# Three weight blocks in place of two through the token quarters of a decoder trunk's opening

## The chip, the cores and the metric

The kernel runs on one core of a Trainium2 chip. The metric is device time in microseconds of one execution; a kernel's time is the median of several runs. Engines have short names: PE is TensorE (matmul), PEld its weight load, DVE is VectorE, ACT is ScalarE, POOL is GpSimd, SP is SyncE, which only issues transfers (DMAs). Each engine works through a queue of its own in written order, and a transfer is issued by SP, ACT or POOL at its place in that engine's queue.

## What is computed

One layer of a hybrid decoder trunk over 1024 prompt tokens and 32 sample tokens of width 1024, cut to what matters here:

```python
h = rmsnorm(x, norm_w)                 # per token: x * rsqrt(mean(x*x) + eps) * w
z = h @ w_in                           # one projection, split into
# q, k, v of a window attention (A), q, k, v of three dilated groups (B),
# pooling inputs (C), gates, merge gates
s = q @ k.T / 8 + bias                 # bias: ALiBi distance and the window's mask
p = softmax(s); o = p @ v              # per head and block of 128 queries
m = sigmoid(ma) * (oa*silu(ga) @ wa) + sigmoid(mb) * (ob*silu(gb) @ wb) + sigmoid(mc) * (oc*silu(gc) @ wc)
y = rmsnorm(x + m @ w_out, final_norm_w)
# further outputs: the last K, V rows of the prompt, and the sample's state
# buffers shifted by four rows, which is a copy from memory to memory
```

## The kernel before, in words

**Data.** A float32 value is kept as two parts, a rounded one (hi) and the rest (lo), so every product takes three matmuls: hi x hi, hi x lo, lo x hi. Tokens stand transposed in `xh` and `xl` (8 blocks of 128 features by 1056 tokens). `w_in` comes as 58 blocks of 1024 x 128. Block 0 is K and block 1 is V of branch A, blocks 2 to 5 are Q of head pairs 0 to 3. A block is loaded to `w_raw` (`w_load`) and split by `w_split`: ACT writes `w_hi`, DVE (in the opening POOL) subtracts to get `w_lo`.

**A projection.** `proj_chunk` multiplies one block with a range of tokens: 24 matmuls into one PSUM bank (tag `pj`, three banks). For blocks 0 and 1 they run part by part: 8 with hi and `xh`, 8 with hi and `xl`, 8 with lo and `xh`; such eight are called a third here. `project(n, ...)` runs a block over three chunks of 384, 384 and 288 tokens.

**The opening** (from L967 on). The 1056 tokens are nine tiles. A tile is loaded (`x_tile`), squared and summed on ACT (`x_sq`, L272) with two small steps on POOL for the reciprocal root (L273, L274), scaled on DVE in two halves (`x_scale`, L282), and turned on PE by eight transposes (`x_turn`, L293), after which ACT copies `xh` out of PSUM (L295) and DVE makes `xl` (L296). Projections need whole quarters: 256, 256, 256 and 288 tokens, two tiles each and three in the last. K and V go through the quarters in turn, and between their chunks the next tiles are squared, scaled and turned. What comes out of a K chunk goes through `evac_k`, which alternates ACT and DVE four times; POOL copies the result to the other half of the partitions. After the opening `project(2)`, Q of pair 0, runs alone.

**Around it.** Two token tiles share each of two pairs of buffers, so SP asks for a tile when an earlier one has been scaled. `make_bias(pair)` has SP load the bias of a pair (256 KB). `state_copy` has POOL issue the memory-to-memory copies of the sample's buffers, 511 KB each; eight of them stand next to each other in POOL's queue behind two small memsets of `up` that end the opening. `later(k, f)` runs `f` after k ticks, a tick being six matmuls of a projection; attention is interleaved with projections by ticks too. Attention of pair 0 starts three ticks into `project(3)`: four matmuls for a block's scores (`emit_s`, L505, two PSUM banks), a minimum with the bias on DVE (L509), an exponential on ACT (L512), transposes (L525) and the product with V (L547).

Of the kernel before, what the change touches and what calls it, by code (L numbers as in the profile page):

```python
# [96 lines left out]
def build(tc, x_p, x_s, w_in, w_pr, w_out, nw, fnw, sink, sinkrow, w_pool, pscale, st_a, st_b1, st_b2, st_b3, st_c,  # L97
# [35 lines left out]
    def w_load(n):  # L133
        if n >= len(seq) or n in raws:
            return
        kind, i = seq[n]
        raw = wr.tile([128, 8, 128], F32, tag="raw", name="w_raw", bufs=2)
        (sp if n == 0 else act).dma_start(out=raw, in_=(w_in if kind == "in" else w_pr)[i])
        raws[n] = raw

    def w_split(n, eng=dve):
        if n >= len(seq) or n in splits:
            return
        w_load(n)
        raw = raws[n]
        if seq[n][0] == "in":
            hi = wr.tile([128, 8, 128], F32R, tag="whi", name="w_hi", bufs=2)
            lo = wr.tile([128, 8, 128], F32R, tag="wlo", name="w_lo", bufs=2)
            act.activation(out=hi, in_=raw, func=AF.Copy)  # L149
            eng.tensor_tensor(out=lo, in0=raw, in1=hi.bitcast(F32), op=ALU.subtract)  # L150
        else:
            hi = wp_pool[0].tile([128, 8, 128], F32R, tag="phi", name="p_hi")
            lo = wp_pool[0].tile([128, 8, 128], F32R, tag="plo", name="p_lo")
            act.activation(out=hi, in_=raw, func=AF.Copy, scale=0.25)
            dve.scalar_tensor_tensor(out=lo, in0=raw, scalar=0.25, in1=hi.bitcast(F32), op0=ALU.mult, op1=ALU.subtract)
        splits[n] = (hi, lo)
# [96 lines left out]
    xh = xtp.tile([128, 8, NT], F32R, tag="xh", name="xh")  # L253
    xl = xtp.tile([128, 8, NT], F32R, tag="xl", name="xl")
    gc1_cm, gc1 = open_pool("gc1")
    up = [gc1.tile([128, 16 + NT], F32, tag=f"c{t}", name=f"up{t}") for t in range(2)]
    at_cm, at0 = open_pool("attn")
    nwb = at0.tile([128, D], F32, tag="bias", name="nwb", bufs=2)

    def x_tile(i):  # L260
        rows = 128 if i < 8 else NS
        xt = at0.tile([128, D], F32, tag=f"q{i % 2}", name="x_nat", bufs=2)
        sp.dma_start(out=xt[:rows], in_=x_p[i * 128:(i + 1) * 128, :] if i < 8 else x_s)
        return xt

    def x_sq(i):
        rows = 128 if i < 8 else NS
        xt = xtiles.pop(i)
        sq = [at0.tile([128, 512], F32, tag="os" if i % 3 == 2 else "e", name="sq", bufs=2 if i % 3 == 2 else 4) for _ in range(2)]
        junk = at0.tile([128, D], mybir.dt.bfloat16, tag="pt", name="junk", bufs=5)  # L270
        ss = at0.tile([128, 2], F32, tag="ss", name="ss", bufs=3)
        act.activation(out=junk[:rows], in_=xt[:rows], func=AF.Square, accum_out=ss[:rows, 0:1])  # L272
        pool.tensor_scalar(out=ss[:rows, 1:2], in0=ss[:rows, 0:1], scalar1=1.0 / D, scalar2=EPS, op0=ALU.mult, op1=ALU.add)  # L273
        pool.tensor_tensor(out=ss[:rows, 0:1], in0=ss[:rows, 1:2], in1=mhalf[:rows], op=ALU.pow)  # L274
        xnorm[i] = xt, sq, ss

    def x_scale(i):
        rows = 128 if i < 8 else NS
        xt, sq, ss = xnorm.pop(i)
        for h in range(2):  # L280
            hs = slice(512 * h, 512 * h + 512)
            dve.scalar_tensor_tensor(out=sq[h][:rows], in0=xt[:rows, hs], scalar=ss[:rows, 0:1], in1=nwb[:rows, hs], op0=ALU.mult, op1=ALU.mult)  # L282
        xscaled[i] = sq

    def x_turn(i):
        rows = 128 if i < 8 else NS
        sq = xscaled.pop(i)
        c0 = i * 128
# [12 lines left out]
    def proj_chunk(n, c0, cn, tag="pj"):  # L301
        hi, lo = splits[n]
        ps = bank(tag)
        parts = ((hi, xh), (hi, xl), (lo, xh))
        order = [(k, p) for p in range(3) for k in range(8)] if n < 2 else [(k, p) for k in range(8) for p in range(3)]
        for step, (k, p) in enumerate(order):
            pe.matmul(ps[:, :cn], lhsT=parts[p][0][:, k, :], rhs=parts[p][1][:, k, c0:c0 + cn], start=(step == 0), stop=(step == 23))  # L307
            if step % 6 == 5:
                yield None
        yield ps  # L310

# [653 lines left out]
        dve.tensor_scalar(out=nsinkrow, in0=sinkrow_sb, scalar1=-1.0, scalar2=None, op0=ALU.mult)  # L965

    warm = bank("o")  # L967
    xtiles[0] = x_tile(0)
    sp.dma_start(out=nwb, in_=bass.AP(tensor=nw.tensor, offset=nw.offset, ap=[[0, 128], [1, D]]))
    xtiles[1] = x_tile(1)  # L970
    w_load(0)
    xtiles[2] = x_tile(2)
    raws[1] = at0.tile([128, 8, 128], F32, tag="bias", name="w_raw1", bufs=2)
    sp.dma_start(out=raws[1], in_=w_in[1])
    xtiles[3] = x_tile(3)
    for _ in range(28):
        pe.transpose(warm[:, 0:128], ident, ident)
    at[0] = at0
# [2 lines left out]
    x_sq(1)  # L981
    x_scale(1)
    x_turn(0)
    w_split(0, pool)
    x_turn(1)
    x_sq(2)
    x_scale(2)
    x_sq(3)
    w_split(1, pool)
    ek, ev = evac_k(0), evac_v(0)  # L990
    nxt_s, nxt_t = 3, 2
    for c0, cn in ((0, 256), (256, 256), (512, 256), (768, 288)):
        for w, e in ((0, ek), (1, ev)):
            if nxt_s < 9:
                if nxt_s + 1 < 9:
                    xtiles[nxt_s + 1] = x_tile(nxt_s + 1)
                x_scale(nxt_s)
                if nxt_s + 1 < 9:
                    x_sq(nxt_s + 1)
                nxt_s += 1  # L1000
            if (c0, w) == (0, 1):
                w_load(2)
            if (c0, w) == (256, 1):
                small_loads()
# [12 lines left out]
    side.append(attention())
    for i in range(4):
        make_bias(i)
        if i >= 2:  # L1020
            flush_attention(i - 2)
        project(2 + i, evac_q(i), 1.6, 2 if i else 0)
    for pr in range(6):
        pair = 4 + pr
        make_bias(pair)
# [445 lines left out]
```

## Time and profile before

| | |
|---|---|
| time, median of 3 runs | 1083.14 us (1082.66 to 1086.08) |
| the profiled execution's own time | 1084.24 us |
| its span in the trace | 1082.5 us |
| PE busy | 1045.4 us, 97% |
| DVE, ACT, POOL busy | 435.5, 343.9, 195.8 us |
| mean granted clock of PE | 0.99 |

The profiled execution is one more run, with the profiler on; its span is what the trace covers. A row of the timeline gives start, duration, engine, line and operation with its output and inputs, and in brackets how long the engine had been idle and what ended that. PE's matmuls are pipelined, so a row's duration is longer than the time for which it holds the engine; the distance between starts tells that.

### The profile page before, as it was taken

What the parts mean: (1) busy time and instruction counts of PE and PEld (TensorE: products, weight loads), DVE (VectorE), ACT (ScalarE), POOL (GpSimd) and SP (SyncE); (2) the same over time, 40 slices, a digit from 0 to 9 for tenths busy, and PEclk for the clock granted to TensorE, in tenths of its full rate; (3) what the DMA queues carried; (4) which work ended last, traced back from release to release, by engine and by line L of the source; (5) the groups of instructions that cost most, each with busy time, mean ns of one, the idle gap of its engine ahead of it and who ended that gap; (6) DMA issues with size and microseconds to landing.
All of it is one profiled execution on the core that took longest, in us unless ns stands there. A gap on an engine that the chain in (4) does not pass through costs nothing.

```text
span 1082.5 us, 18049 instructions
## 1 busy us (share of the span) xinstructions
PE 1045.4 (97%) x7421; PEld 994.4 (92%) x7421; DVE 435.5 (40%) x960; ACT 343.9 (32%) x888; POOL 195.8 (18%) x303
## 2 busy tenths in 40 slices
PE   7999999999999999979999899999999999999996
PEld 7998999999999999968979899999999999998884
DVE  5656654544435343474224641222122221346331
ACT  5456543544535244222211311111112121243221
POOL 5400030211303030300003460311113021111011
PEclk8999999999999999999999999999999999999998
DMA  7241133425254453527568853454143240332221
GB/s 258 79 161 59 60 126 115 149 71 184 70 176 131 124 179 113 160 80 260 194 235 208 256 167 117 164 167 136 60 135 131 83 159 33 92 116 89 100 83 58
DMA packets 54574, 144.42 MB, mean 133 GB/s; under 512 B 13030, under 2 KB 29732, under 8 KB 53156
## 3 DMA queue, kind: packets, MB, share of 16 engines
q1 hardware_dynamic: 41980, 65.28, 19.5%
q0 software_dynamic: 2816, 44.87, 12.2%
q10 hardware_dynamic: 9696, 33.12, 9.9%
q8 instruction: 58, 0.95, 0.4%
q14 instruction: 24, 0.20, 0.1%
HBM read 127.65 MB, written 60.55 MB: 174 GB/s over the span
## 4 chain that ended last, share of the span: by engine, by line
PE 83%; DMA 7%; DVE 5%; ACT 2%; POOL 1%; SPq 1%; issue 1%; POOLq 0%; ACTq 0%; DVEq 0%
PE ps_pj L307 53%; PE ps_pj L1342 5%; PE ps_s L1342 4%; PE ps_s L1207 4%; PE ps_t L1207 4%; PE ps_s L505 3%; PE ps_o L547 3%; PE ps_t L525 2%; DMA w_in<-w_scr 2%; POOL o_in L1134 1%; DMA w_raw<-in_w_in 1%; DMA w_in<-rz_scr 1%; DMA kv<-in_kt_b 1%; PE ps_o L860 1%; DMA o_in<-o_scr 1%
## 5 line engine op out<-in xcount | busy, mean ns | idle before, releaser
L307 PE MATMUL ps_pj<-xh,w_hi 128*128 128x384 f32 (+2 forms) x1408 | 461.7, 335 | 6.4 <-ACT xh L295 3.0
L307 PE MATMUL ps_pj<-xh,w_lo 128*128 128x384 f32 (+2 forms) x1408 | 443.9, 322 | 5.2 <-DVE w_lo L150 5.1
L307 PE MATMUL ps_pj<-xl,w_hi 128*128 128x384 f32 (+2 forms) x1408 | 444.4, 322 | 0.0
L307 PEld LDWEIGHTS ps_pj<-xh,w_hi 128*128 128x128 f32 x1408 | 263.2, 190 | 16.1 <-issue 6.3
L307 PEld LDWEIGHTS ps_pj<-xh,w_lo 128*128 128x128 f32 x1408 | 261.6, 188 | 6.4 <-DVE w_lo L150 6.0
L307 PEld LDWEIGHTS ps_pj<-xl,w_hi 128*128 128x128 f32 x1408 | 262.7, 189 | 0.7 <-issue 0.3
L150 DVE TENSOR_TENSOR w_lo<-w_raw,w_hi 128x1024 fp32r<-128x1024 f32 x55 | 67.3, 1224 | 204.6 <-ACT w_hi L149 197.0
L1216 ACT ACTIVATE mth<-ps_pj 128x384 f32<-128x384 f32 (+1 forms) x72 | 33.4, 464 | 257.3 <-PE ps_pj L307 250.3
L1224 POOL TENSOR_TENSOR m<-m,mth 128x384 f32<-128x384 f32 (+1 forms) x48 | 47.8, 1012 | 275.4 <-DVE mth L1222 274.9
L397 POOL TENSOR_SCALAR k<-k 64x384 fp32r<-64x384 f32 (+1 forms) x44 | 20.1, 458 | 298.4 <-ACT k L393 298.1
L512 ACT ACTIVATE e<-e,nm_b 128x256 f32<-128x256 f32 (+1 forms) x96 | 44.2, 461 | 62.9 <-DVE nm_b L509 62.6
L149 ACT ACTIVATE w_hi<-w_raw 128x1024 fp32r<-128x1024 f32 x57 | 60.1, 1054 | 1.0 <-DMA w_raw<-in_w_in 1.0
L357 DVE SCALAR_TENSOR_TENSOR q<-ps_pj,q 64x384 fp32r<-64x384 f32 (+1 forms) x60 | 30.7, 512 | 60.2 <-ACT q L356 60.1
L505 PE MATMUL ps_s<-k,q 128*128 128x256 f32 x320 | 51.6, 285 | 0.9 <-DVE nm_a L509 0.9
L505 PEld LDWEIGHTS ps_s<-k,q 128*128 128x128 f32 x320 | 45.9, 188 | 1.3 <-issue 1.2
L525 PE MATMUL ps_t<-ident,e 128*128 128x128 f32 x276 | 42.9, 273 | 1.8 <-ACT pt L530 1.1
L1134 POOL TENSOR_TENSOR o_in<-o_in,w_in 128x1024 f32<-128x1024 f32 x10 | 27.9, 2795 | 86.8 <-DMA o_in<-o_scr 62.8
L356 ACT ACTIVATE q<-ps_pj 64x384 fp32r<-64x384 f32 (+1 forms) x60 | 26.8, 447 | 50.4 <-PE ps_pj L307 29.3
L182 POOL DMA_DIRECT2D out_b_s<-in_st_b x84 | 42.2, 507 | 0.0
L512 ACT ACTIVATE e<-e,nm_a 128x256 f32<-128x256 f32 (+1 forms) x64 | 31.1, 487 | 27.9 <-DVE nm_a L509 27.9
L509 DVE CUSTOM_DVE_ANT_0 e<-ps_s,bias 128x256 f32<-128x256 f32 (+1 forms) x96 | 31.9, 371 | 14.9 <-PE ps_s L505 14.2
L525 PEld LDWEIGHTS ps_t<-ident,e 128*128 128x128 f32 x276 | 33.8, 140 | 4.3 <-ACT pt L530 1.9
(240 smaller groups left out, 1323.4 us busy)
## 6 DMA issues: line engine op xcount, KB each, us to landing
out_b_s<-in_st_b POOLq DMA_DIRECT2D x64, 511.0 KB, 6.8
w_raw<-in_w_in ACTq DMA_DIRECT2D x55, 512.0 KB
kv<-in_kt_b SPq DMA_DIRECT2D x16, 512.0 KB
kv<-in_st_b SPq DMA_DIRECT2D x16, 512.0 KB
out_b_s<-in_st_b POOLq DMA_DIRECT2D x16, 508.0 KB, 5.2
o_scr<-os SPq DMA_DIRECT2D x20, 256.0 KB
o_in<-o_scr SPq DMA_DIRECT2D x10, 512.0 KB
x_nat<-in_x_p SPq DMA_DIRECT2D x8, 512.0 KB
```

Of the source, the lines that this page charges most:

```text
L149: act.activation(out=hi, in_=raw, func=AF.Copy)
L150: eng.tensor_tensor(out=lo, in0=raw, in1=hi.bitcast(F32), op=ALU.subtract)
L182: pool.dma_start(out=dst, in_=src)
L307: pe.matmul(ps[:, :cn], lhsT=parts[p][0][:, k, :], rhs=parts[p][1][:, k, c0:c0 + cn], start=(step == 0), stop=(step == 23))
L505: pe.matmul(ps[:, 256 * hd:256 * hd + 256], lhsT=q, rhs=rhs, start=(i == 0), stop=(i == 1))
L512: act.activation(out=e[:, hd, :nk], in_=e[:, hd, :nk], func=AF.Exp, scale=-1.0, bias=nm, accum_out=z)
L525: pe.transpose(tp[:, o:o + 128], e[:, hd, 128 * k:128 * k + 128], ident)
L1134: pool.tensor_tensor(out=t[:, :L], in0=t[:, :L], in1=w[:, :L], op=ALU.mult)
L1207: pe.matmul(pp[:, :cn], lhsT=a[:, k, :], rhs=b[k][:, c0:c0 + cn], start=(step == 0), stop=(step == last))
L1216: act.activation(out=th[:, :cn], in_=ps[:, :cn], func=AF.Tanh, scale=0.5)
L1224: pool.tensor_tensor(out=dst, in0=dst, in1=th[:, :cn], op=ALU.add)
L1342: pe.matmul(banks[c0][:rows, :cn], lhsT=a[:, k, t0:t0 + rows], rhs=wo[k][b][:, c0:c0 + cn], start=(k == 0 and si == 0), stop=(k == 7 and s ...
```

## The change

Block 2 (Q of pair 0) joins K and V in the opening. In the first quarter the three blocks run third by third: hi x `xh` of K, V, Q, then hi x `xl`, then lo x `xh`, with the turns of tiles 2 and 3 between them; in the other quarters chunk by chunk. Blocks 0 to 2 are rounded by `w_first`, on ACT and DVE; block 2's two parts lie in the buffers that `up` takes later. All token tiles have buffers of their own and are asked for at the start. Block 2 is loaded ahead of the third token tile, blocks 3 and 4 within the opening. `project(2)` is gone, and attention still starts in `project(3)`. Within the opening a tick is now a third.

```diff
-    up = [gc1.tile([128, 16 + NT], F32, tag=f"c{t}", name=f"up{t}") for t in range(2)]
+    up = []
...
-        xt = at0.tile([128, D], F32, tag=f"q{i % 2}", name="x_nat", bufs=2)
+        tag, n = (("v", 3), ("v", 3), ("k10", 2), ("k11", 2), ("k20", 2), ("k21", 2), ("q0", 2), ("q1", 2), ("v", 3))[i]
+        xt = at0.tile([128, D], F32, tag=tag, name="x_nat", bufs=n)
...
-        order = [(k, p) for p in range(3) for k in range(8)] if n < 2 else [(k, p) for k in range(8) for p in range(3)]
+        order = [(k, p) for p in range(3) for k in range(8)] if n < 3 else [(k, p) for k in range(8) for p in range(3)]
...
-            if step % 6 == 5:
+            if step % (8 if n < 3 else 6) == (7 if n < 3 else 5):
...
+    def w_first(n):
+        hi, lo = splits[n] if n < 2 else first_w
+        act.activation(out=hi, in_=raws[n], func=AF.Copy)
+        dve.tensor_tensor(out=lo, in0=raws[n], in1=hi.bitcast(F32), op=ALU.subtract)
+        splits[n] = (hi, lo)
+
+    first_w = [gc1.tile([128, 16 + NT], F32R, tag=f"c{t}", name=f"w_first{t}")[:, 0:D].rearrange("p (k c) -> p k c", k=8) for t in range(2)]
...
-    xtiles[2] = x_tile(2)
     raws[1] = at0.tile([128, 8, 128], F32, tag="bias", name="w_raw1", bufs=2)
     sp.dma_start(out=raws[1], in_=w_in[1])
-    xtiles[3] = x_tile(3)
+    raws[2] = wr.tile([128, 8, 128], F32, tag="raw", name="w_raw", bufs=2)
+    sp.dma_start(out=raws[2], in_=w_in[2])
+    for i in range(2, 9):
+        x_tile(i)
...
-    w_split(0, pool)
+    w_first(0)
     x_turn(1)
+    w_first(1)
     x_sq(2)
     x_scale(2)
+    w_first(2)
     x_sq(3)
-    w_split(1, pool)
-    ek, ev = evac_k(0), evac_v(0)
-    nxt_s, nxt_t = 3, 2
-    for c0, cn in ((0, 256), (256, 256), (512, 256), (768, 288)):
-        for w, e in ((0, ek), (1, ev)):
-            if nxt_s < 9:
-                if nxt_s + 1 < 9:
-                    xtiles[nxt_s + 1] = x_tile(nxt_s + 1)
-                x_scale(nxt_s)
-                if nxt_s + 1 < 9:
-                    x_sq(nxt_s + 1)
-                nxt_s += 1
-            if (c0, w) == (0, 1):
-                w_load(2)
-            if (c0, w) == (256, 1):
+    x_scale(3)
+    first_e = (evac_k(0), evac_v(0), evac_q(0))
+    quarters = ((0, 256), (256, 256), (512, 256), (768, 288))
+
+    def norm(i):
+        x_sq(i)
+        x_scale(i)
+
+    c0, cn = quarters[0]
+    runs = [proj_chunk(w, c0, cn) for w in range(3)]
+    for p in range(3):
+        for w in range(3):
+            next(runs[w])
+            if p == 2:
+                first_e[w](c0, cn, next(runs[w]))
+            elif (p, w) in ((0, 1), (1, 1)):
+                x_turn(2 + p)
+    norm(4)
+    w_load(3)
+    for c in range(1, 4):
+        c0, cn = quarters[c]
+        for w in range(3):
+            if w == 0 and c < 3:
+                norm(2 * c + 3)
+            elif w == 1 and c < 3:
+                x_turn(2 * c + 2)
+                norm(2 * c + 4)
+            elif w == 2 and c < 3:
+                x_turn(2 * c + 3)
+            if (c, w) == (2, 2):
+                x_turn(8)
+            if (c, w) == (2, 0):
                 small_loads()
-                raws[3] = up[0][:, 16:16 + D].rearrange("p (k c) -> p k c", k=8)
-                sp.dma_start(out=raws[3], in_=w_in[3])
-            if (c0, w) == (768, 1):
-                w_split(2)
-            run_chunk(w, c0, cn, e, 0)
-            for _ in range(2 if (c0, w) == (512, 1) else 1):
-                if nxt_t < 9:
-                    x_turn(nxt_t)
-                    nxt_t += 1
+            if (c, w) == (3, 0):
+                w_load(4)
+            if (c, w) == (3, 1):
+                w_split(3)
+            run_chunk(w, c0, cn, first_e[w], 0)
+    up += [gc1.tile([128, 16 + NT], F32, tag=f"c{t}", name=f"up{t}") for t in range(2)]
     for t in range(2):
         pool.memset(up[t][:, 0:16], 0.0)
 
     side.append(attention())
-    for i in range(4):
+    make_bias(0)
+    for i in range(1, 4):
         make_bias(i)
         if i >= 2:
             flush_attention(i - 2)
-        project(2 + i, evac_q(i), 1.6, 2 if i else 0)
+        project(2 + i, evac_q(i), 1.6, 2)
```

What this does to the queues is shown at three places. The first is PE's queue in the first quarter, from the turn of tile 1 on; a row with `ps_s` and one with `ps_t` are the two halves of a turn, `x8` is a third. Before:

```order
L293 MATMUL ps_s<-ident,sq 128x128 x4
L293 MATMUL ps_t<-ident,sq 128x128 x4
L307 MATMUL ps_pj<-xh,w_hi 128x256 x8
L307 MATMUL ps_pj<-xl,w_hi 128x256 x8
L307 MATMUL ps_pj<-xh,w_lo 128x256 x8
L293 MATMUL ps_s<-ident,sq 128x128 x4
L293 MATMUL ps_t<-ident,sq 128x128 x4
```

Now, with `w_first_123` and `w_first_124` the two parts of block 2 and `x16` a third of K and one of V:

```order
L308 MATMUL ps_pj<-xh,w_hi 128x256 x16
L294 MATMUL ps_s<-ident,sq 128x128 x4
L294 MATMUL ps_t<-ident,sq 128x128 x4
L308 MATMUL ps_pj<-xh,w_first_123 128x256 x8
L308 MATMUL ps_pj<-xl,w_hi 128x256 x16
L294 MATMUL ps_s<-ident,sq 128x128 x4
L294 MATMUL ps_t<-ident,sq 128x128 x4
L308 MATMUL ps_pj<-xl,w_first_123 128x256 x8
L308 MATMUL ps_pj<-xh,w_lo 128x256 x16
L308 MATMUL ps_pj<-xh,w_first_124 128x256 x8
```

The turn of tile 2 stood behind three thirds of K; now it stands behind one of K and one of V, and the turn of tile 3 behind three more.

The second place is ACT's queue in the third quarter, around the squares of the last tiles (`junk,ss`); `xh` rows are the two halves of a turned tile. Before, from the square of tile 7 on:

```order
L272 ACTIVATE junk,ss<-x_nat 128x1024
L960 DMA sink_sb<-in_sink 128x8
L961 DMA sinkrow_sb<-in_sinkrow 128x2
L962 DMA pw_sb<-in_c_pw 128x34
L963 DMA psc_sb<-in_pscale 128x2
L295 ACTIVATE xh<-ps_s 128x4x128
L295 ACTIVATE xh<-ps_t 128x4x128
L272 ACTIVATE junk,ss<-x_nat 32x1024
L393 ACTIVATE k_236<-ps_pj 64x256
L393 ACTIVATE k_237<-ps_pj 64x256
L295 ACTIVATE xh<-ps_s 128x4x128
L295 ACTIVATE xh<-ps_t 128x4x128
```

Now, with Q's copy of the second quarter ahead:

```order
L357 ACTIVATE q_258<-ps_pj 64x256
L357 ACTIVATE q_259<-ps_pj 64x256
L273 ACTIVATE junk,ss<-x_nat 128x1024
L961 DMA sink_sb<-in_sink 128x8
L962 DMA sinkrow_sb<-in_sinkrow 128x2
L963 DMA pw_sb<-in_c_pw 128x34
L964 DMA psc_sb<-in_pscale 128x2
L394 ACTIVATE k_252<-ps_pj 64x256
L394 ACTIVATE k_253<-ps_pj 64x256
L296 ACTIVATE xh<-ps_s 128x4x128
L296 ACTIVATE xh<-ps_t 128x4x128
L273 ACTIVATE junk,ss<-x_nat 32x1024
```

The square of tile 8 (32 rows) stood ahead of K's copy of the third quarter and now stands behind it, and the square of tile 7 behind Q's copy of the second.

The third place is SP's queue from the last token tiles to attention's start. `up_118` is where block 3 was loaded, `ko` holds K's last rows for the output `out_a_p`. Before:

```order
L263 DMA x_nat<-in_x_p 128x1024 x5
L1006 DMA up_118<-in_w_in 128x1024
L263 DMA x_nat<-in_x_s 32x1024
L467 DMA bias<-in_c_bias 128x2x256
L414 DMA out_a_p<-ko 128x128
L451 DMA out_a_p<-v 128x128
L467 DMA bias<-in_c_bias 128x2x256
```

Now:

```order
L985 DMA w_raw<-in_w_in 128x1024
L264 DMA x_nat<-in_x_p 128x1024 x6
L264 DMA x_nat<-in_x_s 32x1024
L415 DMA out_a_p<-ko 128x128
L468 DMA bias<-in_c_bias 128x2x256 x2
L452 DMA out_a_p<-v 128x128
```

The bias of pair 0 stood ahead of the store of `ko` and now stands behind it, together with that of pair 1.

## Rows read from the trace of the kernel before

**Rows 1.** The page, part 1: busy us (share of the span) and instructions.

```profile
PE 1045.4 (97%) x7421; PEld 994.4 (92%) x7421; DVE 435.5 (40%) x960; ACT 343.9 (32%) x888; POOL 195.8 (18%) x303
```

**Rows 2.** Timeline of PE: start us, us, what [idle before <- releaser].

```profile
10.71 1.11 PE L293 MATMUL ps_s<-ident,sq 128*128 128x128 f32 x4 [2.06 <-DVE sq L282]
...
12.51 1.80 PE L307 MATMUL ps_pj<-xh,w_hi 128*128 128x256 f32 x8
...
24.12 2.08 PE L307 MATMUL ps_pj<-xh,w_hi 128*128 128x256 f32 x8 [2.49 <-ACT xh L295]
...
35.59 1.11 PE L307 MATMUL ps_pj<-xh,w_lo 128*128 128x256 f32 x8
36.54 0.60 PE L293 MATMUL ps_s<-ident,sq 128*128 128x128 f32 x4
...
37.33 1.19 PE L307 MATMUL ps_pj<-xh,w_hi 128*128 128x256 f32 x8
...
48.79 0.44 PE L307 MATMUL ps_pj<-xh,w_hi 128*128 128x384 f32 x1
...
62.52 0.34 PE L307 MATMUL ps_pj<-xh,w_hi 128*128 128x384 f32 x1
...
68.74 0.71 PE L505 MATMUL ps_s<-k,q 128*128 128x256 f32 x4 [0.89 <-DVE nm_a L509]
```

**Rows 3.** Windows: stretch, length, busy us, granted clock, DMA share, GB/s.

```profile
24.10:27.50 3.40, 3.38 (x16) 3.38 (x17) 3.40 (x6) 1.49 (x3) 1.68 (x3) 0.50 0.92 318
...
592.00:595.00 3.00, 2.53 (x14) 2.53 (x15) 2.31 (x2) 1.45 (x2) 2.21 (x1) 1.00 1.04 266
611.00:615.00 4.00, 3.82 (x13) 3.83 (x14) 1.74 (x2) 0.00 (x0) 3.34 (x3) 0.57 0.80 224
```

**Rows 4.** Timeline of ACT, DVE and POOL in the opening.

```profile
4.42 1.06 ACT L272 ACTIVATE junk<-x_nat 128x1024 bf16<-128x1024 f32 x1 [2.20 <-DMA x_nat<-in_x_p]
...
14.24 1.05 ACT L272 ACTIVATE junk<-x_nat 128x1024 bf16<-128x1024 f32 x1
...
14.70 0.55 POOL L274 TENSOR_TENSOR ss<-ss,mhalf 128x1 f32<-128x1 f32 x1
...
15.29 1.41 DVE L282 SCALAR_TENSOR_TENSOR sq<-x_nat,ss,nwb 128x512 f32<-128x512 f32 x2 [1.26 <-POOL ss L274]
...
16.17 0.94 POOL L274 TENSOR_TENSOR ss<-ss,mhalf 128x1 f32<-128x1 f32 x1
...
17.08 2.40 POOL L150 TENSOR_TENSOR w_lo<-w_raw,w_hi 128x1024 fp32r<-128x1024 f32 x1
17.15 3.54 DVE L282 SCALAR_TENSOR_TENSOR sq<-x_nat,ss,nwb 128x512 f32<-128x512 f32 x2 [0.45 <-POOL ss L274]
...
36.74 0.38 ACT L393 ACTIVATE k<-ps_pj 64x256 fp32r<-64x256 f32 x1 [1.72 <-PE ps_pj L307]
...
38.01 0.43 DVE L394 TENSOR_TENSOR k<-ps_pj,k 64x256 fp32r<-64x256 f32 x1 [0.45 <-ACT k L393]
...
48.77 1.23 DVE L150 TENSOR_TENSOR w_lo<-w_raw,w_hi 128x1024 fp32r<-128x1024 f32 x1 [1.38 <-ACT w_hi L149]
```

**Rows 5.** Timeline of SP, POOL, ACT and DVE around the state copies.

```profile
25.16 0.68 SPq L467 DMA_DIRECT2D bias<-in_c_bias  x1
...
48.03 4.13 POOL L182 DMA_DIRECT2D out_b_s<-in_st_b  x8
...
52.66 1.13 ACTq L138 DMA_DIRECT2D w_raw<-in_w_in  x2
...
65.61 1.06 ACT L149 ACTIVATE w_hi<-w_raw 128x1024 fp32r<-128x1024 f32 x1 [0.96 <-DMA w_raw<-in_w_in]
...
67.96 0.35 DVE L509 CUSTOM_DVE_ANT_0 e<-ps_s,bias,nsink 128x128 f32<-128x128 f32 x1
...
86.30 1.05 ACT L149 ACTIVATE w_hi<-w_raw 128x1024 fp32r<-128x1024 f32 x1
```

**Rows 6.** DMA queues, 46 to 70 us: packets, MB, share (q0: the copies).

```profile
q0 software_dynamic: 256, 4.19, 51.8%
```

More of the change, by code (lines that the diff above doesn't have):

```diff
@@ L261, in x_tile @@
         rows = 128 if i < 8 else NS
-        xt = at0.tile([128, D], F32, tag=f"q{i % 2}", name="x_nat", bufs=2)
+        tag, n = (("v", 3), ("v", 3), ("k10", 2), ("k11", 2), ("k20", 2), ("k21", 2), ("q0", 2), ("q1", 2), ("v", 3))[i]
+        xt = at0.tile([128, D], F32, tag=tag, name="x_nat", bufs=n)
         sp.dma_start(out=xt[:rows], in_=x_p[i * 128:(i + 1) * 128, :] if i < 8 else x_s)
-        return xt
+        xtiles[i] = xt
     def x_sq(i):
@@ L967, in build @@
     warm = bank("o")
-    xtiles[0] = x_tile(0)
+    def w_first(n):
[4 more added lines that the diff above has]
+    first_w = [gc1.tile([128, 16 + NT], F32R, tag=f"c{t}", name=f"w_first{t}")[:, 0:D].rearrange("p (k c) -> p k c", k=8) for t in range(2)]
+    for n in range(2):
+        splits[n] = tuple(wr.tile([128, 8, 128], F32R, tag=tag, name="w_" + tag[1:], bufs=2) for tag in ("whi", "wlo"))
+    x_tile(0)
     sp.dma_start(out=nwb, in_=bass.AP(tensor=nw.tensor, offset=nw.offset, ap=[[0, 128], [1, D]]))
-    xtiles[1] = x_tile(1)
+    x_tile(1)
     w_load(0)
-    xtiles[2] = x_tile(2)
     raws[1] = at0.tile([128, 8, 128], F32, tag="bias", name="w_raw1", bufs=2)
     sp.dma_start(out=raws[1], in_=w_in[1])
-    xtiles[3] = x_tile(3)
+    raws[2] = wr.tile([128, 8, 128], F32, tag="raw", name="w_raw", bufs=2)
+    sp.dma_start(out=raws[2], in_=w_in[2])
+    for i in range(2, 9):
+        x_tile(i)
     for _ in range(28):
```

## The prediction, made before the changed kernel had run

> **What bounds the kernel now.** I read the page's head first: TensorE (PE) is busy 1045.4 of 1082.5 us [rows 1], so only what makes PE wait, or run at its lower clock, can move the time. The change touches the first 60 us, so I went to PE's timeline there [rows 2]. The first matmul of the opening's projections stands at 12.51, the first of project(2) at 48.79, and the first of project(3) at 62.52. Between them the reader is to see two holes, 2.06 us ahead of 10.71 and 2.49 us ahead of 24.12, and how long work takes when nothing is missing: a third of a chunk (8 matmuls of 256 columns) holds PE 0.95 us (35.59 to 36.54), the turn of one token tile 0.79 us (36.54 to 37.33). After a hole PE may be slow: from 24.10 to 27.50 the granted clock was 0.50, the lower of its two levels [rows 3], and the 16 matmuls there, two thirds that need 1.9 us, kept PE busy for 3.4; with the start of the next third, a loss of 1.6. That doesn't follow every hole: after 2.12 us at 611 the clock fell (0.57 over four us), after 1.98 us at 592 it stayed at 1.00 [rows 3].
>
> The hole ahead of 24.12 has its cause in another timeline [rows 4]: VectorE's (DVE) scaling of tile 3 took 3.54 us where the same pair took 1.41, while GpSimd's (POOL) rounding of w_lo ran 2.40 us beside it.
>
> A third wait lies outside the opening. The eight state copies are issued from 48.03 on; weights 4 and 5 are asked for at 52.66, and ScalarE (ACT) could start to round weight 4 at 65.61 only, after waiting for the transfer [rows 5]. DVE's first minimum for attention was queued behind its subtraction, and PE stood 0.89 us ahead of 68.74 [rows 2].
>
> **What goes.** Q of pair 0 (project(2)) moves into the opening. Its 96 matmuls stay: 3 quarters of 3 x 0.95 plus one of 3 x 1.07 (288 columns for 256) is 11.8, and the 13.7 from 48.79 to 62.52 hold that, ten transposes (1.1) for K's and V's rows and a wait for weight 2. What could be won is holes that Q's work fills. Without any, PE needs from 12.5 on 36 thirds (27 x 0.95 + 9 x 1.07 = 35.3), six and a half turns (5.8), 0.8 for the first third at the lower clock and 0.45 for a V transpose that now falls inside: the end would be at 54.9, and 0.65 of transposes are still to come. Against 62.52 that is 7.0 us, the most the opening can give. The token tiles' own buffers let their loads run ahead; ACT waited for one only at the first squares (4.42 [rows 4]), which nothing here moves: 0.
>
> **Which holes come.** I walked the five queues in their written order with the durations of [rows 4] (square 1.05 and 0.19 to read its sum; POOL's two steps 0.83, or 1.5 beside a DVE instruction that reads two SBUF tensors, as the 0.94 against 0.55 shows; half a scaling 0.70; a K or Q copy out of PSUM, which alternates ACT and DVE four times, 1.70 from 36.74 to 38.44; weight rounding 1.23 on DVE). The same walk of the old order puts project(2) at 48.82 (row: 48.79) and the third chunk at 23.85 (row: 24.12). In the new order it finds:
> - Turn 2 stands on PE behind V's first third, which ends at 15.1. ACT now rounds w_hi of weight 1 before it squares tile 2, so the square starts at 14.0 (its transfer is the seventh; the seventh of before was there by 14.24, where its square starts [rows 4]). Square to 15.2, POOL beside w_lo on DVE to 16.7, half a scaling: 17.5. PE waits 2.4, and 0.25 more for the second half.
> - Turn 4: ACT reaches the square of tile 4 only after Q's copy of the first quarter, 27.6. Then 1.24, 0.83 and 0.70: PE waits from 29.1 to 30.5, and 0.25.
> - Turn 8 stands ahead of Q's third quarter. Q's second quarter ends at 38.3; its copy on DVE waits for the scaling of tile 6 and the two xl, so ACT is free for the square of tile 7 at 40.5; DVE scales it until 44.0, and only then comes K's copy, behind which ACT has xh of tile 6 and then the square of tile 8 (45.8). POOL and DVE bring its first half at 48.6. PE finished turn 7 at 45.9: it waits 2.8 and 0.45.
> Smaller ones make 0.3. The three weight roundings on DVE are in this walk; the 3.54 is gone. The walk ends at 62.0, with the V transpose 62.5, so with 0.65 still to do the opening is **0.6 us later** than before, if the clock stays up. The holes of 2.4 and 2.8 are as long as those after which it fell (2.06, 2.12, 2.49) or longer; I take both as falls, 1.6 each: **+3.2** (bounds 0 and 3.2; at 1.98 it didn't fall).
>
> **What is late next.** Weight 4 is now asked for in the fourth quarter, ahead of the copies: the 0.89 goes, **-0.9**. Weights 5 and 6 meet the copies, but are wanted only at project(4): weight 5 was rounded at 86.30 [rows 5], 23.8 after project(3)'s start; hidden. The dearest part is bias of pair 0. Before, SP issued it at 25.16, 40 us ahead of its use [rows 5]. Now SP has the store of K's last rows ahead of it, which waits for the transposes after the opening's last matmul (T). So bias goes out at about T+1.3, when POOL, released by the same matmul, has begun the eight copies at T+0.35. Attention wants it at about T+4.6: 0.65 of transposes, three ticks of six 384-column matmuls (1.07 each, by the third's 0.95) and a block's scores (0.5). DVE's in-order queue stops there, and behind it wait the other minima, with them ACT's exponentials, and the copies of project(3)'s Q. PE can still run a tick and the scores of a second block, then no PSUM bank for scores is free: it stands at the third, about T+5.9.
> The cost of that transfer is bounded by rows. Alone it might cost nothing: the first token tile, twice the bytes, was there 4.4 us from the span's start [rows 4]. The nearest row is weight 4: issued at 52.66 into the same eight copies, it was there at 65.6, 17.5 us after the first copy's issue. Its 128 rows of 4 KB met copies that move in 128 rows of 32 KB (4.19 MB [rows 6]), and it landed when they had run dry. Bias has 256 rows of 1 KB, more and smaller, and 64 KB of K rows ahead in its queue. So I take 17.5 after the first copy too: T+17.9, 0.8 more until the first minimum is out (67.96 to 68.74 [rows 2, 5]), less 5.9: PE stands **12.8 us** (bounds 0 and 14). If only the 12.9 us of weight 4's own flight count, it is 9; if half the bytes take half that, 4. A hole this long is followed by the lower clock: **+1.6**.
> [...]
>
> **Sum.** 0.6 + 3.2 - 0.9 + 12.8 + 1.6 = +17.3 on the profiled execution's 1084.24, which lies 1.1 above the median of the runs (1083.14): 1101.5, or 1100 as a median. Two matmul sequences further on shift against attention by a tick; I give that nothing, and 2 us either way in the range.
>
> **Rivals.**
> - Bias gets an equal share of bytes: half of the 318 GB/s that moved at 24 to 27 us [rows 3] carries 256 KB in 1.6 us, on top of what a transfer needs alone, T+6 or so, 0 to 1.3 us of stall. For it: nothing here shows a transfer of 1 KB rows beside copies. Against it: weight 4. Time 1084.2 + 0.6 + 3.2 - 0.9 + 0.7 - 1.1 = 1087; with neither clock fall 1083.5, no change to be told. [...]
> - Half the delay: bias needs half of weight 4's flight, stall 4 and a clock fall: 1092.
> - The other side: the holes don't come. This turns on turn 8 and turn 2: if ACT and DVE reach their squares about 2 us earlier than I walk (an overlap of the K and Q copies, say, where [rows 4] shows them alternate) and bias is in time, 3.5 to 7 us of the opening are won and 0.9 behind it: 1075 to 1079. For it: the 3.54 on DVE is truly gone. Against: the old order's walk fits within 0.3 us.
> - The change doesn't do what it says: Q moves, but the opening only gets longer by as much, and bias is hidden: 1083, within the 0.3%.
>
> **Chances.** Late bias in full (stall 9 to 14) 0.55, half 0.15, equal share 0.17 (of which a third with the clock up, no change), holes gone 0.07, no change 0.06. A measurement of this kernel tells 0.3% (3.2 us) from no change. Faster 0.07; same 0.06 + 0.06 = 0.12, and a little of the faster case's edge, 0.13; slower 0.80. Predicted 1100 us. The range reaches from no change, 1083, to the upper bounds of stall and shift, 1104; the likeliest case alone is 1095 to 1104.
>
> **What would show it.** In the new profile: PE idle of about 2.4 and 2.8 us ahead of turns 2 and 8 and a granted clock near 0.5 for three us behind each; scaling pairs at 1.4 with none at 3.5; no ACT wait for weight 4; the first attention minimum on DVE some 10 us late, released by the bias transfer, and PE idle as long, with the copies in flight. I am wrong if that minimum runs within 2 us of its scores, if project(3) starts before 60, or if the clock stays up throughout.

## The result and the profile after

The changed kernel takes 1100.07 us (median of 4 runs, 1097.77 to 1104.44) where the kernel before, run beside it, takes 1083.77: a ratio of 1.0145, 95% interval 1.0118 to 1.0172. It is slower, by 16 us. The profiled execution took 1101.05 us with a span of 1099.3.

The page of the changed kernel, part 1 (answers to [rows 1]): PE's busy time grew by 6 us, though it has no more columns to multiply (the 24 matmuls more are block 2 in four quarters instead of three chunks, for the same 1056 tokens); the span grew by 16.8.

```profile
PE 1051.3 (96%) x7445; PEld 1000.4 (91%) x7445; DVE 442.0 (40%) x964; ACT 344.6 (31%) x890; POOL 190.5 (17%) x301
```

Timeline of PE in the changed kernel, from the first turns to attention's third block of scores (answers to [rows 2]; line numbers are one higher):

```profile
10.49 0.87 PE L294 MATMUL ps_s<-ident,sq 128*128 128x128 f32 x4 [1.41 <-DVE sq L283]
...
12.05 3.20 PE L308 MATMUL ps_pj<-xh,w_hi 128*128 128x256 f32 x16
17.38 0.88 PE L294 MATMUL ps_s<-ident,sq 128*128 128x128 f32 x4 [2.13 <-DVE sq L283]
...
18.78 2.06 PE L308 MATMUL ps_pj<-xh,w_first 128*128 128x256 f32 x8
...
31.66 0.66 PE L294 MATMUL ps_s<-ident,sq 128*128 128x128 f32 x4 [1.06 <-DVE sq L283]
32.32 0.66 PE L294 MATMUL ps_t<-ident,sq 128*128 128x128 f32 x4
32.73 1.19 PE L308 MATMUL ps_pj<-xh,w_hi 128*128 128x256 f32 x8
...
50.56 0.40 PE L294 MATMUL ps_s<-ident,sq 32*128 32x32 f32 x4 [3.00 <-DVE sq L283]
51.22 0.40 PE L294 MATMUL ps_t<-ident,sq 32*128 32x32 f32 x4 [0.26 <-DVE sq L283]
51.55 1.92 PE L308 MATMUL ps_pj<-xh,w_first 128*128 128x256 f32 x8
...
66.07 0.43 PE L308 MATMUL ps_pj<-xh,w_hi 128*128 128x384 f32 x1
...
83.43 1.20 PE L506 MATMUL ps_s<-k,q 128*128 128x256 f32 x4 [11.40 <-DVE nm_a L510]
```

The reader is to see four holes. Three are in the opening, ahead of the turns of tiles 2, 4 and 8; project(3) starts at 66.07 instead of 62.52. The fourth, 11.40 us, is new and stands ahead of attention's third block. The windows of the same trace (columns as in [rows 3], here PE alone) give the granted clock behind the holes of 2.13, 3.00 and 11.40 us: 0.53, 0.52 and 0.50.

```profile
17.40:21.00 3.60, 3.60 (x18) 0.53 0.39 139
51.60:55.00 3.40, 3.40 (x18) 0.52 0.00 0
...
83.40:89.00 5.60, 5.57 (x21) 0.50 0.26 93
```

Who is late is told by the timeline of the other engines around 67 us (answers to [rows 5]), and by one piece of the chain that ended last:

```profile
66.31 4.12 POOL L182 DMA_DIRECT2D out_b_s<-in_st_b  x8
66.67 0.36 SPq L415 DMA_DIRECT2D out_a_p<-ko  x1
67.13 1.34 SPq L468 DMA_DIRECT2D bias<-in_c_bias  x2
82.65 0.35 DVE L510 CUSTOM_DVE_ANT_0 e<-ps_s,bias,nsink 128x128 f32<-128x128 f32 x1 [12.25 <-DMA bias<-in_c_bias]
...
104.23 1.05 ACT L149 ACTIVATE w_hi<-w_raw 128x1024 fp32r<-128x1024 f32 x1
```

```profile
67.13 15.35 DMA bias<-in_c_bias
```

Bias of pair 0 is asked for at 67.13, 0.82 behind the first state copy, and lands 15.35 us later. DVE's first minimum waits for it, and PE, out of PSUM banks, waits for DVE.

The row at 104.23 is the rounding of weight 5; it stood at 86.30 before [rows 5]. That is a sharper meter than the time: **17.9 us later**, with nothing between but the opening and project(3). The same row is given below for every kernel, as its lag.

### The profile page after: what moved, and what is told of

Its sections match the earlier page's. It is cut to its first block, busy times and chain, and to the rows that moved or that the text cites. A ratio compares the mean times of both kernels' runs of the same rounds, so it can differ in the third digit from the quotient of the medians.

```text
span 1099.3 us, 18089 instructions
## 1 busy us (share of the span) xinstructions
PE 1051.3 (96%) x7445; PEld 1000.4 (91%) x7445; DVE 442.0 (40%) x964; ACT 344.6 (31%) x890; POOL 190.5 (17%) x301
## 4 chain that ended last, share of the span: by engine, by line
PE 83%; DVE 7%; DMA 4%; ACT 2%; POOL 1%; issue 1%; SPq 0%; ACTq 0%; POOLq 0%; DVEq 0%
PE ps_pj L308 54%; PE ps_pj L1371 5%; PE ps_s L1371 4%; PE ps_s L1236 4%; PE ps_t L1236 4%; PE ps_s L506 3%; PE ps_o L548 3%; PE ps_t L526 2%; DMA bias<-in_c_bias 1%; DVE w_lo L150 1%; DVE sq L283 1%; PE ps_s L743 1%; PE ps_o L861 1%; DMA kv<-in_kt_b 1%; DVE glo L1184 1%
## 5 line engine op out<-in xcount | busy, mean ns | idle before, releaser
L308 PE MATMUL ps_pj<-xh,w_hi 128*128 128x384 f32 (+2 forms) x1384 | 454.5, 335 | 3.8 <-DVE t L1094 3.1
L308 PE MATMUL ps_pj<-xh,w_lo 128*128 128x384 f32 (+2 forms) x1384 | 437.6, 323 | 1.9 <-DVE w_lo L150 1.9
L308 PE MATMUL ps_pj<-xl,w_hi 128*128 128x384 f32 (+2 forms) x1384 | 438.5, 324 | 0.2 <-DVE xl L297 0.2
L308 PEld LDWEIGHTS ps_pj<-xh,w_hi 128*128 128x128 f32 x1384 | 259.7, 191 | 13.3 <-issue 6.9
L308 PEld LDWEIGHTS ps_pj<-xh,w_lo 128*128 128x128 f32 x1384 | 258.3, 189 | 2.2 <-DVE w_lo L150 2.2
L308 PEld LDWEIGHTS ps_pj<-xl,w_hi 128*128 128x128 f32 x1384 | 259.0, 190 | 1.2 <-DVE xl L297 0.4
L150 DVE TENSOR_TENSOR w_lo<-w_raw,w_hi 128x1024 fp32r<-128x1024 f32 x55 | 71.5, 1300 | 203.2 <-ACT w_hi L149 203.0
L506 PE MATMUL ps_s<-k,q 128*128 128x256 f32 x320 | 52.5, 288 | 11.4 <-DVE nm_a L510 11.4
```

The source lines that it names most:

```text
L506: pe.matmul(ps[:, 256 * hd:256 * hd + 256], lhsT=q, rhs=rhs, start=(i == 0), stop=(i == 1))
```

## The experiments

The times of the first four stand beside 1085.15 us for the kernel before on the same chip, those of the other four beside 1087.4. The ratios are estimates with their 95% intervals and lie up to 0.2% from the quotients of these medians.

**1. Bias early.** One line is moved:

```diff
     side.append(attention())
-    make_bias(0)
...
             if (c, w) == (3, 0):
+                make_bias(0)
                 w_load(4)
```

> The changed kernel with one load moved: bias of pair 0 is asked for ahead of the fourth quarter's K chunk, so it stands ahead of the store of K's rows in SP's queue and some 10 us ahead of the state copies. Theory (the late bias is the stall): PE's 11.4 us before the third block's scores go, and the slow clock behind them (about 2 us); first minimum on DVE within 2 us of its scores; time 1086 to 1088. Rival (the stall would only pass to another transfer that the copies hold up, bias of pair 1 or weight 5): a new wait of 5 us or more within project(3) or project(4), time 1092 to 1100.

1088.14 us, ratio 1.0029 (1.0009 to 1.0049). The first minimum of its timeline has no wait, and weight 5's rounding comes 5.2 us later than before instead of 17.9 (1.2 of the 5.2 is a longer clock fall: tile 2's turn starts only 0.1 later than in the changed kernel, at 17.47, but the granted clock from 17.4 to 21 us is 0.50 for 0.53, the xl thirds of K and V take 2.92 us (20.91 to 23.83) where they took 2.08 there (20.63 to 22.71), and project(3) starts at 67.24).

```profile
71.69 0.35 DVE L510 CUSTOM_DVE_ANT_0 e<-ps_s,bias,nsink 128x128 f32<-128x128 f32 x1
...
91.48 1.05 ACT L149 ACTIVATE w_hi<-w_raw 128x1024 fp32r<-128x1024 f32 x1
```

Some 12 to 14 us are the late bias (12.6 by the two ratios, 12.7 by the lags, 13.9 without the longer fall), and nothing else takes its place: the longest wait of PE behind it, up to 108 us, is 0.74 us. What stays is the opening.

**2. No copies beside it.** Bias stays as late as in the changed kernel; the first eight copies go elsewhere:

```diff
-        project(2 + i, evac_q(i), 1.6, 2)
+        project(2 + i, evac_q(i), 1.6, 0)
...
-        project(n, evac_k(pair), rate)
-        project(n + 1, evac_v(pair), rate)
+        project(n, evac_k(pair), rate, (0, 4, 4, 2, 2, 2)[pr])
+        project(n + 1, evac_v(pair), rate, (2, 4, 2, 2, 2, 2)[pr])
...
-        project(n + 2, evac_q(pair), rate)
+        project(n + 2, evac_q(pair), rate, (2, 4, 2, 2, 2, 2)[pr])
```

> The changed kernel with the first eight state copies taken away from the opening's end and given back between the projections of pair 4's V and pair 6's K; bias of pair 0 stays as late as in the changed kernel. Theory (the copies' bytes ahead of bias make it late): bias lands 3 to 4 us after its issue instead of 15.35, PE's stall is 0 to 2 us, time 1086 to 1090. Rival (what makes it late is its place in SP's queue, behind the store of K's rows, or its 256 rows of 1 KB themselves): flight stays above 10 us, stall above 6 us, time 1094 to 1101.

1087.83 us, ratio 1.0028 (1.0009 to 1.0047). PE, SP, DVE and ACT in its timeline:

```profile
65.90 0.42 PE L308 MATMUL ps_pj<-xh,w_hi 128*128 128x384 f32 x1
...
66.97 1.32 SPq L468 DMA_DIRECT2D bias<-in_c_bias  x2
...
70.36 0.35 DVE L510 CUSTOM_DVE_ANT_0 e<-ps_s,bias,nsink 128x128 f32<-128x128 f32 x1
...
84.01 0.66 PE L548 MATMUL ps_o<-pt,v 128*64 128x128 f32 x8 [0.74 <-DVE pt L533]
...
88.24 0.63 PE L526 MATMUL ps_t<-ident,e 128*128 128x128 f32 x4 [0.44 <-DVE pt L533]
...
90.15 1.05 ACT L149 ACTIVATE w_hi<-w_raw 128x1024 fp32r<-128x1024 f32 x1
```

Issued at the same place, behind the same store, bias is there within 3.4 us. So the place in SP's queue is harmless without the copies, and the copies are harmless without the late bias (experiment 1): it takes both. The lag is 3.85.

**3. The copies in smaller rows, first try.**

```diff
-                dst, src = (t.rearrange("(a b) -> a b", a=16) for t in (dst, src))
+                dst, src = (t.rearrange("(a b) -> a b", a=128 if len(copies) >= 78 else 16) for t in (dst, src))
```

> The changed kernel with the same eight state copies cut into 128 rows of 4 KB each instead of 16 of 32 KB; nothing else differs, the bytes are the same. Theory A (an engine of the DMA goes round its queues row by row, so a row of 1 KB of bias is held up by one row of a copy): with rows an eighth as long, bias lands 3 to 6 us after its issue, stall 0 to 3 us, time 1086 to 1091. Theory B (bias lands when the copies have run dry, whatever their rows): flight 14 to 17 us and stall 10 to 13 us as in the changed kernel, time 1098 to 1103. [...]

1102.79 us, ratio 1.0146 (1.0119 to 1.0173); the minimum stands at 82.83 after a wait of 13.69. That looks like theory B, but the edit didn't reach the hardware. The DMA packets of this kernel from 50 to 110 us, and of them the copies' queue (packets, MB, share), which has the same 256 as [rows 6]:

```profile
DMA packets 2083, 7.25 MB, mean 121 GB/s; under 512 B 288, under 2 KB 1312, under 8 KB 1952
...
q0 software_dynamic: 256, 4.19, 19.1%
```

Only 131 packets of the window have 8 KB or more, in this kernel as in the changed one. So the 4.19 MB still moved as some 128 pieces of 32 KB (the other half of the 256 packets is small): by these counts rows that lie next to each other were joined again. The run tells nothing about row size, and experiment 5 was made for that.

**4. Bias early, and the opening in another order.** In the first quarter K and V run two thirds each before tile 2 is turned, and every later tile is squared and scaled a place earlier:

```diff
-    for p in range(3):
-        for w in range(3):
+    for p, w in ((0, 0), (0, 1), (1, 0), (1, 1), (0, 2), (1, 2), (2, 0), (2, 1), (2, 2)):
...
+        elif (p, w) == (1, 1):
+            x_turn(2)
+            norm(4)
+        elif (p, w) == (1, 2):
+            x_turn(3)
+    norm(5)
...
+            if (c, w) == (1, 0):
+                norm(6)
             elif w == 1 and c < 3:
                 x_turn(2 * c + 2)
-                norm(2 * c + 4)
+                if c == 1:
+                    norm(7)
             elif w == 2 and c < 3:
                 x_turn(2 * c + 3)
+                if c == 1:
+                    norm(8)
```

> The changed kernel with bias of pair 0 early and the opening's order rewritten: in the first quarter K and V run their hi and xl thirds before the turn of tile 2, and Q's first two thirds fill the time to the turn of tile 3; tiles 4 to 8 are squared and scaled one place earlier each. Theory (what the opening lost to before are PE's holes ahead of turns 2, 4 and 8, 2.13 + 1.06 + 3.26 us, and two falls of the clock of about 1.6 each): all three under 0.5 us, project(3)'s first matmul at 57 to 59 instead of 66.07, time 1077 to 1081, faster than before the change. Rival (the holes move to another place of the opening, as ACT and DVE have the same work in a shorter time): project(3) starts at 61 or later, time 1083 to 1087.

1083.9 us, ratio 0.9985 (0.9965 to 1.0005); lag -1.9. Theory and rival were both half right. PE's timeline:

```profile
17.62 0.64 PE L294 MATMUL ps_s<-ident,sq 128*128 128x128 f32 x4 [0.16 <-DVE sq L283]
...
25.66 1.18 PE L308 MATMUL ps_pj<-xh,w_hi 128*128 128x256 f32 x8 [1.15 <-DVE k L395]
...
38.72 1.33 PE L308 MATMUL ps_pj<-xl,w_hi 128*128 128x256 f32 x8 [1.61 <-DVE xl L297]
...
46.19 0.43 PE L294 MATMUL ps_s<-ident,sq 32*128 32x32 f32 x4 [0.58 <-DVE xl L297]
...
60.15 0.43 PE L308 MATMUL ps_pj<-xh,w_hi 128*128 128x384 f32 x1
```

The holes ahead of turns 2 and 4 are gone, that of turn 8 is down to 0.58, and the granted clock is 1.00 in the windows from 17.4 to 21, 24 to 28 and 51.6 to 55 us. But DVE now scales a tile ahead of K's copy and of an `xl` that PE wants sooner, and PE stands 1.15 and 1.61 us there. Project(3) starts 5.9 us earlier than in the changed kernel, not 7 to 9.

**5. Copies in rows that can't be joined.** Each of the first eight copies takes every other group of seven token rows:

```diff
+    for kv in range(2):
+        for r0 in (0, 1022):
+            for s in range(2):
+                copies.append(tuple(t.rearrange("(j s r) c -> s j r c", s=2, r=7)[s] for t in (b3_s[0, kv, r0:r0 + 1022, :], st_b3[0, kv, 4 + r0:4 + r0 + 1022, :])))
```

> The kernel with copies cut into 128 contiguous rows moved the same 256 packets of 16 KB as the changed kernel, so rows that lie next to each other were joined again and it told nothing of the rows' size. Here the first eight copies are made of rows that can't be joined: each takes every other group of seven token rows, 73 pieces of 7 KB (one copy's gaps are the next one's rows), same bytes within 1 KB, bias as late as in the changed kernel. Theory A (engines take turns between queues piece by piece: 16 packets of a copy against 16 rows of bias on each engine is why bias landed when the copies ran dry): about 36 pieces of copies an engine against 16 rows of bias, so bias lands after about 45 per cent of the copies, 6 to 9 us after its issue, stall 2 to 5 us, time 1089 to 1094. Theory B (bytes asked for earlier go first, whatever the pieces): flight 14 to 17 us, stall 10 to 13 us, time 1098 to 1103.

**6. Bias in larger rows.** The unused half of pair 0's bias is loaded too, so each partition's row is 4 KB in one:

```diff
+        if pair == 0:
+            nb = 2
         sp.dma_start(out=t[:, :, 0:nb, :], in_=c_bias[pair].rearrange("p (a b k) -> p a b k", a=2, b=2)[:, :, 0:nb, :])
```

> The changed kernel, but bias of pair 0 is loaded whole, as 128 rows of 4 KB (512 KB) in place of 256 rows of 1 KB (256 KB); the half that is added isn't used. Copies and order stay. Theory A (turns piece by piece): 8 rows an engine instead of 16 against the same 16 packets of copies, so twice the bytes land earlier, 7 to 10 us after the issue, stall 3 to 6 us, time 1090 to 1095. Theory B (bytes asked for earlier go first): flight 15 to 17.5 us, stall 11 to 14 us, time 1099 to 1103.

Timeline of experiment 5, POOL, SP, DVE and ACT, and its copies' queue from 60 to 95 us:

```profile
67.33 4.39 POOL L186 DMA_DIRECT2D out_b_s<-in_st_b  x8
...
68.15 1.33 SPq L472 DMA_DIRECT2D bias<-in_c_bias  x2
...
78.38 0.35 DVE L514 CUSTOM_DVE_ANT_0 e<-ps_s,bias,nsink 128x128 f32<-128x128 f32 x1 [6.97 <-DMA bias<-in_c_bias]
...
99.48 1.05 ACT L149 ACTIVATE w_hi<-w_raw 128x1024 fp32r<-128x1024 f32 x1
```

```profile
q0 software_dynamic: 768, 4.19, 31.6%
```

And of experiment 6:

```profile
68.40 4.13 POOL L182 DMA_DIRECT2D out_b_s<-in_st_b  x8
...
69.22 1.11 SPq L470 DMA_DIRECT2D bias<-in_c_bias  x2
...
77.36 0.35 DVE L512 CUSTOM_DVE_ANT_0 e<-ps_s,bias,nsink 128x128 f32<-128x128 f32 x1 [4.87 <-DMA bias<-in_c_bias]
...
97.85 1.05 ACT L149 ACTIVATE w_hi<-w_raw 128x1024 fp32r<-128x1024 f32 x1
```

From the first copy's issue to DVE's start it is 16.3 us in the changed kernel, 11.1 with the copies in 768 packets (584 pieces of 7 KB and small ones), and 9.0 with bias in 128 rows, though it then has twice the bytes. PE stands 6.1 and 4.0 us instead of 11.4, and the lags are 13.2 and 11.6. Theory B, by which bytes asked for earlier go first, is out: neither edit would have helped. Fewer rows of bias help, and so do smaller pieces of the copies: for half the rows of bias the delay is 0.55 of what it was, for three times the packets of the copies 0.68. Theory A held in size for experiment 6 (8.1 us from issue to start and a stall of 4.0, where it gave 7 to 10 and 3 to 6) and not for 5 (10.2 and 6.1, where it gave 6 to 9 and 2 to 5).

Count and size of the pieces change together in both, so what each does has to come from the counts of packets. Changed kernel, 72 to 82.5 us (q0: the copies, q10: ACT's weights, q1: SP's loads and stores):

```profile
q0 software_dynamic: 166, 2.71, 73.7%
q10 hardware_dynamic: 169, 0.63, 17.5%
q1 hardware_dynamic: 176, 0.16, 5.8%
```

Here the queues moved nearly the same number of packets, with 17 times the bytes in q0 as in q1. Turns piece by piece would give that; it is the author's reading of these counts, and no row shows an engine going from one queue to the next. Read so, bias's wait is its count of rows, each held up for as long as a copy's piece takes. But not all of bias went so: from 70.5 to 72 q1 moved 186 packets, 0.19 MB, in a burst. If experiment 5 has such a burst too, which was not shown, three times the packets shorten only the part behind it and not the 4.9 us from the issue (67.13) to 72, and its delay can't fall to a third. Which of the 16 engines had the last row, the trace doesn't tell, so the landing itself is not worked out from turns.

The times are 1099.29 us for experiment 5 (1.0100, 1.0060 to 1.0141, two runs) and 1094.68 for 6 (1.0050, 1.0028 to 1.0073). The first misses theory A's 1089 to 1094, although weight 5 is rounded 4.7 us earlier than in the changed kernel. Experiment 5 and the kernel before round the last weight of the input projection at

```profile
957.24 1.05 ACT L149 ACTIVATE w_hi<-w_raw 128x1024 fp32r<-128x1024 f32 x1
```

```profile
937.73 1.05 ACT L149 ACTIVATE w_hi<-w_raw 128x1024 fp32r<-128x1024 f32 x1
```

so its lag grew from 13.2 to 19.5. That arose between 480 and 660 us, where PE is busy for 162.7 of 180 us (before 170.3): it waits once for ACT, 4.9 us, which it doesn't before, and 3.9 us for the sample's transfers, before 1.7. The changed kernel's own lag went from 17.5 to 16.8 in the same stretch.

**7. The kernel before, with one part of the change alone.** `w_split(0, pool)` and `w_split(1, pool)` become `w_split(0)` and `w_split(1)`.

> The kernel before with one part of the change alone: w_lo of weights 0 and 1 is made on VectorE instead of GpSimd. Theory (GpSimd's 2.40 us beside the scaling of tile 3 made that 3.54 us and with it PE's hole of 2.49 us and the slow thirds behind it): scaling pairs 1.4 to 1.6, the hole under 1 us, granted clock 1.00 behind it, project(2) 2 to 4 us earlier than 48.79, time 1079 to 1082 beside 1083 to 1085. Rival (DVE has two times 1.2 us more to do and the hole stays, from DVE being late instead): project(2) within 1 us of 48.79, time the same within 0.2 per cent.

1084.67 us, ratio 0.9972 (0.9948 to 0.9996); lag -2.55. DVE's scaling of tile 3, PE's second quarter, and the window behind it:

```profile
17.52 1.41 DVE L282 SCALAR_TENSOR_TENSOR sq<-x_nat,ss,nwb 128x512 f32<-128x512 f32 x2
```

```profile
22.36 1.22 PE L307 MATMUL ps_pj<-xh,w_hi 128*128 128x256 f32 x8 [1.23 <-ACT xh L295]
...
46.27 0.44 PE L307 MATMUL ps_pj<-xh,w_hi 128*128 128x384 f32 x1
```

```profile
24.00:28.00 4.00, 4.00 (x34) 1.00 0.45 145
```

The 3.54 us are 1.41, the hole is 1.23 instead of 2.49, the clock stays at 1.00, and project(2) starts 2.5 us earlier. The theory holds, but for a hole a little larger than it said (1.23, not under 1).

**8. The order of 4, with DVE's queue mended.** Squares stay early, but DVE scales tiles 4 to 8 behind the copies and `xl` that PE waits for; tile 8 is turned inside Q's third quarter; the small loads move to the fourth:

```diff
+            x_turn(2)
+            x_sq(4)
...
+            x_turn(3)
+            x_sq(5)
+        elif (p, w) == (2, 1):
+            x_scale(4)
+    x_scale(5)
...
+                for step, ps in enumerate(proj_chunk(w, c0, cn)):
+                    if step == 1:
+                        x_turn(8)
```

> As the kernel with bias early and the opening's order rewritten, whose PE still stood 1.15 us for K's bank (DVE scaled tile 4 ahead of K's copy), 1.61 us for xl of tile 5 (behind the scaling of tile 7) and 0.75 us ahead of the turn of tile 8. Here squares stay early on ACT, but DVE scales tiles 4 to 8 one place later, behind the copies and xl that PE waits for; the turn of tile 8 stands between Q's second and last third of the third quarter; the small loads go out in the fourth quarter. Theory (each hole was a DVE queue order): PE's waits from 12 us to project(3) sum to under 1.2 us, clock 1.00 from 16 us on, project(3) at 56.5 to 58.5 instead of 60.15, time 1079.5 to 1082 where before shows 1084 to 1085, ratio 0.995 to 0.997. Rival (what the opening wins is given back in the middle of the kernel, where project spacing moved by up to 4 us between kernels): project(3) at 57, but time within 1 us of the earlier order's, ratio 0.998 to 0.999.

1079.15 us, ratio **0.9925** (0.9902 to 0.9948): faster than before the change. PE's timeline holds two small holes, and one of 0.20, between 12 us and project(3):

```profile
17.58 0.63 PE L294 MATMUL ps_s<-ident,sq 128*128 128x128 f32 x4 [0.81 <-DVE sq L283]
...
25.10 1.18 PE L308 MATMUL ps_pj<-xh,w_hi 128*128 128x256 f32 x8 [0.61 <-DVE k L395]
...
56.60 0.42 PE L308 MATMUL ps_pj<-xh,w_hi 128*128 128x384 f32 x1
```

Project(3) starts 5.9 us earlier than before and 9.5 earlier than in the changed kernel, and the lag is -5.5; the holes sum to 1.6 where the theory wanted 1.2. The ratio is better than the theory's 0.995 to 0.997: it makes 8 us, of which the opening explains 5.5.

## Why the prediction was right, point by point

| step | predicted | measured |
|---|---|---|
| holes ahead of turns 2, 4, 8 | 2.65, 1.65, 3.25 | 2.13, 1.06, 3.26 |
| project(3) starts, with two clock falls | 65.7 | 66.07 |
| wait for weight 4 | gone, -0.9 | gone |
| opening and project(3) without the bias | +2.9 | +3.9 (experiment 2) |
| bias there, from the first copy's issue | 17.5 | 16.3 |
| PE's stall | 12.8 | 11.4 |
| clock fall behind it | 1.6 | 2.5 |
| sum | 17.3 | 17.9 at weight 5, 16.8 at the end |

- **The opening's holes** came where the walk put them and for its reasons: POOL's two steps took 0.84 beside DVE's rounding, against 0.19 with DVE idle (before, at 14.43), and 0.55 behind it (1.5 predicted), and the square of tile 8 stood behind K's copy. Ahead of the second halves of turns 2 and 4 no row shows a wait, and these two holes are 0.5 and 0.6 us shorter than in the walk; but turn 4 holds PE for 1.07 us (31.66 to 32.73) where 0.79 is usual, so some 0.3 of it is there all the same. That the holes are queue order and no lack of work is shown by experiment 8, which does the same work in an opening that ends 9.5 us earlier.
- **The gain that the part with w_lo brings** was in the walk and is shown alone by experiment 7: 2.5 us. The change as a whole loses it again in its own holes.
- **Two clock falls** came, behind 2.13 and 3.00 us, as taken. Of the 2152 half-us windows of this trace from 2 to 1078 us 2078 read a granted clock of 1.00, 60 one of 0.50, and 14 lie between, each next to a change from one to the other.
- **+3.9 against +2.9.** From the rows of experiment 2: 3.4 later at project(3) (65.90), 0.65 of transposes, less 0.89, make 3.1. In the 0.7 that is left stand two waits of PE for DVE's copy of the transposed softmax weights (`pt`), 0.74 ahead of 84.01 and 0.44 ahead of 88.24; before, PE has none between 68.74 and 86.30. The prediction saw that attention would shift by a tick about there and gave it nothing. That the shift makes these waits is likely and not shown.
- **The late bias** is shown by experiments 1 and 2. The mechanism (asked for behind the store of K's rows, and so into the copies) held. The term was 1.4 too large, since bias came 1.2 earlier behind the first copy. That weight 4's flight fitted so well is luck in part: experiment 6 puts a load of weight 4's shape, 128 rows of 4 KB, in bias's place, and that is there 9.0 behind the first copy, not 17.5; bias has twice the rows. The reason given, that a transfer lands when the copies "had run dry", fits weight 4 (the copies' queue moved 0.29 MB from 62 to 64 us and under 0.01 from 64 to 65.6) and bias here (all of its 4.19 MB lie between 66.3 and 82.65). It doesn't fit the other sizes: when bias landed in experiments 5 and 6, all queues together had moved about 3.4 and 2.9 MB since the first copy, so copies were still to come. The fall behind the stall was mis-sized, 1.6 for 2.5: the 17.93 of lag, less experiment 2's 3.85, less 0.17 by which its opening was shorter, less 11.40. The 1.6 came from a hole with two thirds behind it, and here the clock was low for longer (0.50 up to 89).
- **How bias went through.** The changed kernel's trace shows two parts. From 70.5 to 72 us q1 moved 186 packets, some 12 for each of 16 engines, while q0 moved 29. From 72 to 82.5 the three queues went nearly one for one (176, 169 and 166 packets), and the 256 rows took 15.35 us in all. With half as many rows and twice the bytes (experiment 6) bias came 7.4 us earlier behind the first copy, 9.0 for 16.3.
- **Rivals.** Equal share and half delay fell with the 11.4. A stall as long as half delay's came with half the rows (experiment 6, 4.0 us); with late bias and the copies beside it no run shows one as short as equal share's. The holes did come.
- **Two slips in the working.** "Its 96 matmuls stay" should be 72 before and 96 now, of the same 1056 columns; and six and a half turns of 0.79 are 5.1, not 5.8, so the most that the opening could give is 7.7 and not 7.0. The forecast of 1100 adds up neither.
- **1100.0 for 1100.07** is better than the working, by luck: +0.6 at weight 5, then -1.1 in the middle of the kernel, where experiment 5 moved by 6 us for no reason in the opening. The 2 us "either way" that the prediction gave that stretch were too few.

## What to carry to other kernels

When a loop is unrolled into another order, look for the loads that stood ahead of a late store in an issuing queue and now stand behind it: here a load that was 40 us early became the only one on the path, and the bulk copies that were harmless beside it are what it then waited for (15.35 us, of which PE stood 11.40). Filling PE's holes with more matmuls paid here only with the vector engines' queues written for it, what PE waits for ahead of what merely could run (a ratio of 0.9925 in experiment 8 against 1.0029 in experiment 1, both with bias early). And read a change of a few us at a landmark right behind it, before unrelated stretches add their own scatter (6.3 us in experiment 5).

## What was not expected of the hardware

- A small transfer beside memory-to-memory copies was delayed by its count of rows more than by its bytes: 256 KB in 256 rows of 1 KB took 15.35 us, 512 KB in 128 rows of 4 KB 8.1 (69.22 to 77.36), and the first at most 3.4 without the copies. Queues of very different rows moved 166, 169 and 176 packets in the same 10.5 us.
- A copy described as 128 rows of 4 KB moved as the same 256 packets as one of 16 rows of 32 KB (131 packets of 8 KB or more in both windows), until its rows had gaps between them (768 packets).
- Behind holes of about the same length the clock fell or not: 0.53 behind 2.13 us in the changed kernel, 0.59 behind 2.07 in experiment 2, and 1.00 behind 1.85 in experiment 3 and behind 1.96 (10.5 to 14 us) in experiment 8.
